# Six modulation vectors of a transformer block: one reduction moved from TensorE to VectorE, another into the feed-forward

## The chip, the cores and the metric

The kernel runs on one core of a Trainium2 chip. The core has five engines with a queue each: TensorE (PE, matrix products, with PEld as its weight load), VectorE (DVE), ScalarE (ACT), GpSimd (POOL) and SyncE (SP, which issues most transfers). Each queue is worked off in order; engines wait for each other by semaphores. The metric is the time of one execution on the device in microseconds.

## The reference

Two transformer blocks stand behind each other, for 256 tokens of width 1024, all in fp32. The first block has two kinds of attention (MoBA, and a gated delta rule that solves a triangular system), an output projection and a mixture of 32 experts with a router. The second block is modulated: six vectors of 1024 numbers are made from a condition `c` and are used as shift, scale and gate.

```python
mod = (jax.nn.silu(c) @ w_mod[l] + b_mod[l])[:, None, :]
mod_c = (jax.nn.silu(c_ctx) @ w_mod[l] + b_mod[l])[None, None, :]
sh1, sc1, g1, sh2, sc2, g2 = jnp.split(mod, N_MOD, axis=-1)
csh1, csc1, cg1, csh2, csc2, cg2 = jnp.split(mod_c, N_MOD, axis=-1)
h = _modulate(_rms_norm(x, norm1_g[l]), sh1, sc1)      # h * (1 + scale) + shift
hc = _modulate(_rms_norm(ctx, norm1_g[l]), csh1, csc1)
...
h2 = _modulate(_rms_norm(x_new, norm2_g[l]), sh2, sc2)
x = x_new + g2 * _swiglu(h2, w_gate[l], w_up[l], w_down[l])
```

The weight `w_mod` has 1024 x 6144 numbers, 24 MB. Of the six vectors of the context condition only the first two (shift and scale of the first norm) reach an output, so vectors 2 to 5 are needed for one condition alone. The hidden layer of the feed-forward has 2816 columns, which are worked through as 11 blocks of 256.

## The kernel before, in words

Weights come in blocks of 1 MB ([128, 2048] fp32) into a ring of nine slots (`load_block`); SP issues the loads in the order of use, and a load waits until its slot is free. For the exact products a block is split into a high and a low part (`split_w`): ACT writes the high part in two pieces of 1024 columns, DVE the low part in four of 512 (for some blocks POOL does). A product is then three matmuls (`mm3`).

Stage a makes the projections of block 1 while the delta rule's triangular inverse goes on. The inverse is a chain of short steps. First a loop over four heads makes the matrices `pkq` (a product of the keys `kn` with keys and queries), from which DVE makes `BT` and `QT`. Then seven levels follow, for two halves (`blk`) by turns: PE makes `pu`, DVE multiplies by a mask (`U`), PE multiplies again, DVE subtracts (`T`) and transposes (`W`); the last two levels have copies (`X`, `T64`, `Wf`) instead. Behind the levels come products `py` and `pb` with copies `yy` and a subtraction `vt`. The matmuls of this chain are short and each waits for DVE; so that PE has work, `fill(n)` puts `FILL[n]` steps of the projections (one `mm3` each) between them. From `PE.start()` on, which stands ahead of the levels, PE's order is as written; the other engines' order is made by a scheduler from the program, with `after(a, b)` as a bare order (a stands behind b on its engine, no semaphore).

The six modulation vectors are a generator, `mod_steps`, that yields after each weight block. `more_mod(n)` advances it by n yields; `MODS[:14]` says by how many after each projection, `MODR` after each level, `MODS[14:]` after each step of MoBA. A vector is four blocks of 1 MB. For each, PE takes the silu'd condition (`sil`, 32 columns: two conditions, 16 copies each) as weights and multiplies 256 columns at a time into four column groups of one PSUM tile, `pmod`: 32 matmuls a vector. Then DVE transposes it (line 397), adds the bias (line 398), and for the two scales multiplies by the norm's gain (line 400). All of it goes on in stage a, from the first projections to the end of the levels.

Stage c (router and experts, 96 MB of weights) follows, then stage d, block 2. In its feed-forward `ffn_up(b)` makes gate and up products `pfg` and `pfu` of a hidden block (48 matmuls each, on weights `fg` and `fu`, split into `fgh`, `fgl`, `fuh`, `ful`), ACT the silu (`fsg`, line 1801), DVE the product; `ffn_down(b)` multiplies by `fd` into four accumulators `pf`. The input is made by `mod_T`: DVE scales (`mt`, line 1470), ACT shifts into the high part (`hif`, line 1471), DVE makes the low part (`lof`, line 1472), for eight slices. The last gate g2 has to lie along the free axis, equal in all rows: `row_bc` makes that by 8 matmuls (`prb`) and two copies on ACT (`g2B`, line 1526), ahead of the first `ffn_up`; with `RBH` the copies stand behind the last `hif`.

Of the kernel before, what the change touches and what calls it, by code (L numbers as in the profile page):

```python
# [9 lines left out]
F32 = mybir.dt.float32  # L10
# [3 lines left out]
ALU = mybir.AluOpType  # L14
# [3 lines left out]
P = 128  # L18
D = 1024
# [86 lines left out]
def tile_kernel(ctx: ExitStack, tc: tile.TileContext, I, out, dbg=None):  # L106
# [99 lines left out]
    def bc(ap, n):  # L206
        return ap[..., None].to_broadcast(list(ap.shape) + [n])
# [172 lines left out]
    def mod_steps():  # L380


        for n in range(6):
            p = psm([P, 256], "pmod", "mo")
            wm = w_mod[:, n * D:n * D + D].rearrange("(p k) c -> p k c", k=8)
            for i in range(4):
                w = load_block(wm[:, 2 * i:2 * i + 2], "wmod")
                for kk in range(2):
                    for j in range(4):
                        m = PE.matmul(p[32 * j:32 * j + 32], lhsT=sil[:, 2 * i + kk].rearrange("p a b -> p (a b)"),  # L390
                                  rhs=w[:, kk, 256 * j:256 * j + 256], start=i + kk == 0, stop=i + kk == 4)
                        if kk + j == 0:
                            S_["mod"] = S_["mod0"] = m
                if i < 3:
                    yield
            part = tmp_([P, 8, 32], "part", "part")
            DVE.transpose(part, p.rearrange("p (c k) -> p k c", k=8))
            DVE.tensor_tensor(mod[:, n], part[:, :, 0::16], bc(bmc[:, n], 2), op=ALU.add)
            if n in (1, 4):
                DVE.scalar_tensor_tensor(mod[:, n], mod[:, n], 1.0, bc((gN1, gN2)[n // 4], 2), op0=ALU.add, op1=ALU.mult)  # L400
            yield

    MODA = MODS[:14]
# [3 lines left out]
    def more_mod(n=1):  # L407
        on, PE.on = PE.on, False
        for _ in range(n):
            before = S_.get("mod")  # L410
            next(mods, None)
            if S_.get("mod") is not before:
                if S_["nmod"] < MBEH and "pj1" in S_:
                    after(S_["mod0"], S_["pj1"])
                S_["nmod"] += 1
        PE.on = on
# [170 lines left out]
    for h in range(4):  # L587
# [8 lines left out]
        for dst, rr in ((BT[:, :, h], kn), (QT[h], gT["q", h])):  # L596
# [4 lines left out]
            DVE.scalar_tensor_tensor(dst[:, 0:2], src[:, 0:2], bt[:, 0, h:h + 1], dec[h][:, 0:2], op0=ALU.mult, op1=ALU.mult)  # L601
            DVE.scalar_tensor_tensor(dst[:, 2], src[:, 2], bt[:, 1, h:h + 1], dec[h][:, 2], op0=ALU.mult, op1=ALU.mult)

# [25 lines left out]
    def level(blk, n):  # L629
# [14 lines left out]
        Wn = ic("W")  # L644
        DVE.transpose(Wn.rearrange("p a b -> p (a b)"), Tn.rearrange("p a b -> p (a b)"))
        T[blk], W[blk] = Tn, Wn
# [27 lines left out]
    def level_64(blk):  # L674
# [3 lines left out]
        X = T64[blk]  # L678
        DVE.tensor_copy(X[64:128], px[64:128])
        yield  # L680
# [35 lines left out]
    fill(9)  # L716
    DVE.tensor_copy(yy[1], py)
    ob = aa([P, 2, 4, P], "zg", "ob", bufs=2)
# [1050 lines left out]
    pow_ins = S_["pow"]  # L1769

    with tc.issue_after(S_["rp"].ins):
        g2B = row_bc(mod[:, 5, :, 0], ring_tile("g2B", F32)[:, 0:D], ("mo", "sm"))
    if RBH:
        for i in S_["rbc"]:
            after(i, S_["hin"])
    rb_ins = S_["rb"]

    mt_ins, sq_ins, lo_ins = S_["mt"], S_["sq"], S_["lo"]
# [38 lines left out]

    prev = ffn_up(0)
    for b in range(1, 12):
        nxt = ffn_up(b) if b < 11 else None  # L1820
        ffn_down(b - 1, *prev)
        prev = nxt
# [9 lines left out]

MODR = [2, 2, 2, 2, 2, 2]
MODS = [0, 1, 2, 0, 1, 0, 1, 0, 2, 2, 2, 2, 2, 1, 0, 0, 0, 0]
IFU = 4
# [19 lines left out]
IC = 8  # L1855
FILL = [3] * 7 + [6] * 5 + [0, 2, 2]
START = 2
# [18 lines left out]
JKA = (True, True)  # L1876
RBH = True

# [28 lines left out]
```

## Time and profile before

| what | value |
|---|---|
| time, median of 3 runs | 831.15 us (830.29 to 833.35) |
| profiled execution | 835.07 us, span 833.3 us |
| mean granted clock of TensorE | 0.959 of full speed |
| PE busy | 758.9 us, 91% |
| PEld busy | 608.6 us, 73% |
| DVE busy | 425.8 us, 51% |
| ACT busy | 302.0 us, 36% |
| POOL busy | 108.2 us, 13% |
| moved by DMA | 201.21 MB, mean 241 GB/s |

The shares are means over stages with different limits; the table of stretches among the rows below shows them apart. A row of the timeline reads: start, busy time, engine, line, operation, output and input names, shape, how many instructions, and in brackets how long the engine was idle before it and whom it waited for. Matmuls overlap in the pipe, so pace is read from starts. Each fp32 matmul leaves two records (`x384` for the 192 matmuls of pmod); those of split parts leave one.

### The profile page before, as it was taken

Reading aid. Unit: us, or ns where it says so; the run is one execution under the profiler, and the core shown is the slowest. Engines: PE = TensorE matmul, PEld = TensorE weight load, DVE = VectorE, ACT = ScalarE, POOL = GpSimd, SP = SyncE. Lnnn points to the kernel's source line nnn. Section 1 sums busy time; section 2 is a strip of 40 time slices with the busy share of each in tenths; the row PEclk is TensorE's granted clock in tenths of the full one; section 3 lists DMA queues with packets and bytes.
Section 4 is the critical chain, followed back from the end, with each engine's and each line's share of the span. In section 5 each row is a group of like instructions: output and inputs, shape, how many; then the busy total and the mean of one; then the engine's idle time right before and its main releaser. Section 6 shows DMA issues by size and latency. Waiting matters only on the chain.

```text
span 833.3 us, 15024 instructions
## 1 busy us (share of the span) xinstructions
PE 758.9 (91%) x6276; PEld 608.6 (73%) x6276; DVE 425.8 (51%) x938; ACT 302.0 (36%) x533; POOL 108.2 (13%) x94
## 2 busy tenths in 40 slices
PE   7999999999799878697888999799988999999997
PEld 6887887966645425274654889688867999999996
DVE  4766553564612114003224788888655545545545
ACT  5532233443410010001114554488525343443441
POOL 5011000152000000000000566300122000000000
PEclk9999999999799989799898999799998999999999
DMA  7999778577589999999998317011442654655201
GB/s 213 357 386 390 283 280 298 203 288 319 206 341 419 420 417 419 391 409 409 409 396 284 116 22 206 2 51 52 152 152 79 225 197 161 199 187 171 97 2 50
DMA packets 87590, 201.21 MB, mean 241 GB/s; under 512 B 15496, under 2 KB 63040, under 8 KB 75232
## 3 DMA queue, kind: packets, MB, share of 16 engines
q1 hardware_dynamic: 87328, 200.12, 65.1%
q8 instruction: 50, 0.82, 0.4%
q0 software_dynamic: 192, 0.11, 0.1%
q14 instruction: 20, 0.16, 0.1%
HBM read 199.27 MB, written 1.05 MB: 240 GB/s over the span
## 4 chain that ended last, share of the span: by engine, by line
PE 39%; DMA 6%; DVE 6%; issue 3%; POOL 2%; ACT 1%; SPq 1%; DVEq 0%; POOLq 0%; ACTq 0%
PE pfu L99 8%; PE pfg L99 7%; PE pf L99 7%; PE sc L99 3%; DMA ed<-in_w_down_dram 3%; DMA kv<-in_w_in_dram 2%; PE po L99 2%; PE ptp L102 2%; PE pyd L99 2%; PE pqa L99 1%; PE pqb L99 1%; POOL rq L218 1%; PE ckbp L99 1%; PE pgu L99 1%; DMA lat<-in_w_in_dram 1%
## 5 line engine op out<-in xcount | busy, mean ns | idle before, releaser
L99 PE MATMUL pfu<-hif,fuh 128*128 128x256 f32 x176 | 50.7, 288 | 1.6 <-ACT fuh L185 1.6
L99 PE MATMUL pfu<-hif,ful 128*128 128x256 f32 x176 | 50.7, 288 | 0.9 <-POOL ful L192 0.9
L99 PE MATMUL pfu<-lof,fuh 128*128 128x256 f32 x176 | 50.6, 287 | 0.0
L99 PE MATMUL pyd<-ed,hid 128*32 128x512 f32 x256 | 42.0, 667 | 7.1 <-DMA ed<-in_w_down_dram 2.4
L99 PE MATMUL pfg<-hif,fgh 128*128 128x256 f32 x160 | 45.7, 286 | 0.0
L99 PE MATMUL pfg<-lof,fgh 128*128 128x256 f32 x160 | 45.7, 285 | 0.0
L99 PE MATMUL pfg<-hif,fgl 128*128 128x256 f32 x160 | 45.6, 285 | 0.0
L192 DVE TENSOR_TENSOR fdl<-fd,fdh 128x512 fp32r<-128x512 f32 x44 | 27.5, 687 | 28.9 <-ACT fdh L185 28.9
L99 PE MATMUL pgu<-eu,xg 128*32 128x256 f32 x512 | 35.7, 402 | 3.9 <-DMA eu<-in_w_up_dram 3.9
L1377 ACT ACTIVATE sg<-pgu,r1s 128x256 f32<-128x256 f32 x8 | 3.8, 474 | 94.7 <-PE pgu L99 70.9
L99 PEld LDWEIGHTS pfu<-hif,fuh 128*128 128x128 f32 x176 | 34.6, 197 | 1.8 <-ACT fuh L185 1.8
L185 ACT ACTIVATE fuh<-fu 128x1024 fp32r<-128x1024 f32 x22 | 22.1, 1052 | 38.2 <-issue 28.6
L99 PE MATMUL pgu<-eg,xg 128*32 128x256 f32 x512 | 34.2, 385 | 1.6 <-DVE sg L1378 1.1
L185 ACT ACTIVATE fdh<-fd 128x1024 fp32r<-128x1024 f32 x22 | 22.1, 1052 | 36.9 <-issue 36.1
L99 PEld LDWEIGHTS pfu<-hif,ful 128*128 128x128 f32 x176 | 34.6, 196 | 1.1 <-POOL ful L192 1.1
L99 PE MATMUL pf<-fdl,fh 128*128 128x512 f32 x88 | 35.1, 399 | 0.0
L1404 DVE TENSOR_TENSOR yl<-pyd,yh 128x512 fp32r<-128x512 f32 x16 | 11.1, 691 | 46.3 <-ACT yh L1403 35.9
L99 PE MATMUL pf<-fdh,fh 128*128 128x512 f32 x88 | 34.7, 394 | 0.0
L99 PEld LDWEIGHTS pfu<-lof,fuh 128*128 128x128 f32 x176 | 34.6, 197 | 0.0
L99 PE MATMUL pf<-fdh,fl 128*128 128x512 f32 x88 | 34.0, 392 | 0.0
L99 PEld LDWEIGHTS pyd<-ed,hid 128*32 128x32 f32 x256 | 9.7, 120 | 33.2 <-issue 22.0
L192 DVE TENSOR_TENSOR fgl<-fg,fgh 128x512 fp32r<-128x512 f32 x40 | 27.7, 753 | 9.1 <-ACT fgh L185 9.1
(716 smaller groups left out, 2185.2 us busy)
## 6 DMA issues: line engine op xcount, KB each, us to landing
eg<-in_w_gate_dram SPq DMA_DIRECT2D x32, 1024.0 KB, 17.5
eu<-in_w_up_dram SPq DMA_DIRECT2D x32, 1024.0 KB, 19.8
ed<-in_w_down_dram SPq DMA_DIRECT2D x32, 1024.0 KB, 15.4
wmod<-in_w_mod_dram SPq DMA_DIRECT2D x24, 1024.0 KB, 10.6
fg<-in_w_gate_dram SPq DMA_DIRECT2D x11, 1024.0 KB, 5.4
fu<-in_w_up_dram SPq DMA_DIRECT2D x11, 1024.0 KB, 5.3
fd<-in_w_down_dram SPq DMA_DIRECT2D x11, 1024.0 KB, 5.0
kv<-in_w_in_dram SPq DMA_DIRECT2D x5, 1024.0 KB, 15.2
```

The costliest lines, as they stand in the source:

```text
L99: return self._keep(self.engine.matmul(*args, **kwargs))
L102: return self._keep(self.engine.transpose(*args, **kwargs))
L185: S_["hi"] = ACT.activation(hf[:, s], vf[:, s], AF.Copy)
L192: i = (POOL if c in pool else DVE).tensor_tensor(lf[:, s], vf[:, s], hf[:, s], op=ALU.subtract)
L218: S_["pow"] = POOL.tensor_tensor(r, v, mhalf[:, :n], op=ALU.pow)
L1377: ACT.activation(sg, pgu[:, 0], AF.Silu, scale=r1s[:, u:u + 1])
L1404: DVE.tensor_tensor(yl, py, yh, op=ALU.subtract)
```

## The change

Vectors 0 and 1 (both conditions) stay on PE. Vectors 2, 3 and 4 go by `mod_sum`: DVE multiplies the first row block by its number of the condition in place (`TENSOR_SCALAR`, line 414 of the new kernel), and adds each other row block times its number to it (`SCALAR_TENSOR_TENSOR`, line 416): 128x512 each, 16 a vector. The first weight block's own slot holds the sums, so it stays taken until the vector is done. Then the 128 partitions are summed by 8 matmuls with one column of ones (`pmod`, [128, 8]), and the bias is added (line 431, 433). The first sum of each block is put behind the last step of the chain by `after` (`S_["hold"]`, which is set to the last of `BT`/`QT`, `W`, `X`, `yy`). Vector 5 is summed by the same `mod_rows` inside the feed-forward, one block at each of b = 3, 4, 5 and 6; at b = 7 two matmuls of 128x512 with ones sum the partitions and spread the result over all rows, and DVE adds a bias row that a broadcast transfer has brought. `row_bc` for g2 and `RBH` go. `MODR`, `MODS` and the first seven of `FILL` change: from the third level on four steps of the projections instead of three stand at each place.

```diff
 
-        for n in range(6):
+        for n in range(5):
+            if n > 1:
+                yield from mod_sum(n)
+                continue
             p = psm([P, 256], "pmod", "mo")
...
             DVE.tensor_tensor(mod[:, n], part[:, :, 0::16], bc(bmc[:, n], 2), op=ALU.add)
-            if n in (1, 4):
-                DVE.scalar_tensor_tensor(mod[:, n], mod[:, n], 1.0, bc((gN1, gN2)[n // 4], 2), op0=ALU.add, op1=ALU.mult)
+            if n == 1:
+                DVE.scalar_tensor_tensor(mod[:, n], mod[:, n], 1.0, bc(gN1, 2), op0=ALU.add, op1=ALU.mult)
             yield
+    def mod_rows(n, i, acc):
+
+        w = load_block(w_mod[:, n * D:n * D + D].rearrange("(p k) c -> p k c", k=8)[:, 2 * i:2 * i + 2], "wmod")
+        for kk in range(2):
+            for c in range(2):
+                cs = slice(512 * c, 512 * c + 512)
+                f = sc2t[:, 0, 2 * i + kk:2 * i + kk + 1]
+                if i + kk == 0:
+                    S_["sum0"] = DVE.tensor_scalar(w[:, 0, cs], w[:, 0, cs], f, None, op0=ALU.mult)
+                else:
+                    m = DVE.scalar_tensor_tensor((acc or w)[:, 0, cs], w[:, kk, cs], f, (acc or w)[:, 0, cs], op0=ALU.mult, op1=ALU.add)
+                    if kk + c == 0:
+                        S_["sum0"] = m
+        return acc or w
+
+    def mod_sum(n):
+
+        acc = None
+        for i in range(4):
+            acc = mod_rows(n, i, acc)
+            if i < 3:
+                yield
+        p = psm([P, 8], "pmod", "mo")
+        for k in range(8):
+            PE.matmul(p[:, k:k + 1], lhsT=acc[:, 0, k::8], rhs=ones1, start=True, stop=True)
+        DVE.tensor_tensor(mod[:, n, :, 0], p, bmc[:, n], op=ALU.add)
+        if n == 4:
+            DVE.scalar_tensor_tensor(mod[:, n, :, 0], mod[:, n, :, 0], 1.0, gN2, op0=ALU.add, op1=ALU.mult)
+        yield
 
...
-            before = S_.get("mod")
+            before, sum_ = S_.get("mod"), S_.get("sum0")
             next(mods, None)
+            if S_.get("sum0") is not sum_ and "hold" in S_:
+                after(S_["sum0"], S_["hold"])
...
         Wn = ic("W")
-        DVE.transpose(Wn.rearrange("p a b -> p (a b)"), Tn.rearrange("p a b -> p (a b)"))
+        S_["hold"] = DVE.transpose(Wn.rearrange("p a b -> p (a b)"), Tn.rearrange("p a b -> p (a b)"))
...
-    with tc.issue_after(S_["rp"].ins):
-        g2B = row_bc(mod[:, 5, :, 0], ring_tile("g2B", F32)[:, 0:D], ("mo", "sm"))
-    if RBH:
-        for i in S_["rbc"]:
-            after(i, S_["hin"])
-    rb_ins = S_["rb"]
-
+    g2 = ring_tile("g2B", F32)
+    g2B, b2B = g2[:, 0:D], g2[:, D:2 * D]
...
     prev = ffn_up(0)
+    acc = None
     for b in range(1, 12):
         nxt = ffn_up(b) if b < 11 else None
+        if b in GB:
+            if acc is None:
+                bcast_dma(b2B, I["b_mod_2"][0, 5 * D:6 * D], D)
+            acc = mod_rows(5, GB.index(b), acc)
+        if b == GB[-1] + 1:
+            for nh in range(2):
+                ns = slice(nh * 512, nh * 512 + 512)
+                p = psm([P, 512], "pg2", ("mo", "sm")[nh])
+                PE.matmul(p, lhsT=ones1.to_broadcast([P, P]), rhs=acc[:, 0, ns], start=True, stop=True)
+                DVE.tensor_tensor(g2B[:, ns], p, b2B[:, ns], op=ALU.add)
         ffn_down(b - 1, *prev)
...
-MODR = [2, 2, 2, 2, 2, 2]
-MODS = [0, 1, 2, 0, 1, 0, 1, 0, 2, 2, 2, 2, 2, 1, 0, 0, 0, 0]
+MODR = [1, 1, 1, 1, 1, 1]
+MODS = [0, 1, 2, 1, 1, 1, 1, 1, 0, 0, 1, 1, 2, 2, 0, 0, 0, 0]
...
-FILL = [3] * 7 + [6] * 5 + [0, 2, 2]
+FILL = [3, 3, 4, 4, 4, 4, 4] + [6] * 5 + [0, 2, 2]
...
-RBH = True
+GB = (3, 4, 5, 6)
```

The new lines `S_["hold"] = ...` stand in the same way at `QT`, `X` and `yy`.

The order on DVE in the inverse. Before, at the level where `wmk1` is split (L634 is `U`, L643 `T`, L645 `W`, L397 the vectors' transposition):

```order
L634 TENSOR_TENSOR U<-pu,lvl 128x128 x2
L543 SCALAR_TENSOR_TENSOR zg<-zg,wz1p 128x2x256
L643 TENSOR_TENSOR T<-T,pu 128x128
L555 TENSOR_TENSOR zg<-zg,gnorm 128x1024
L192 TENSOR_TENSOR wmk1l<-wmk_1456,wmk1h 128x512
L645 STREAM_TRANSPOSE W<-T 128x128
L192 TENSOR_TENSOR wmk1l<-wmk_1456,wmk1h 128x512
L397 STREAM_TRANSPOSE part<-pmod 128x256
L192 TENSOR_TENSOR wmk1l<-wmk_1456,wmk1h 128x512 x2
L643 TENSOR_TENSOR T<-T,pu 128x128
L398 TENSOR_TENSOR mod<-part,bmc 128x16
L645 STREAM_TRANSPOSE W<-T 128x128
```

After, at the end of the levels (L719 is `Wf`, the sums L414 and L416, L742 the copy `yy`, L431 the bias of a vector):

```order
L416 SCALAR_TENSOR_TENSOR wmod<-wmod,sc2t 128x512 x2
L719 TENSOR_SCALAR Wf_916<-pu 64x4x64
L416 SCALAR_TENSOR_TENSOR wmod<-wmod,sc2t 128x512 x3
L719 TENSOR_SCALAR Wf_920<-pu 64x4x64
L416 SCALAR_TENSOR_TENSOR wmod<-wmod,sc2t 128x512 x3
L192 TENSOR_TENSOR wmv1l<-wmv_1873,wmv1h 128x512 x2
L416 SCALAR_TENSOR_TENSOR wmod<-wmod,sc2t 128x512
L192 TENSOR_TENSOR wmv1l<-wmv_1873,wmv1h 128x512 x2
L416 SCALAR_TENSOR_TENSOR wmod<-wmod,sc2t 128x512
L742 COPY yy_1766<-py 128x512
L416 SCALAR_TENSOR_TENSOR wmod<-wmod,sc2t 128x512 x3
L431 TENSOR_TENSOR mod<-pmod,bmc 128x8
```

One to three sums stand in front of each step of the chain; in the rows before, only splits, the gate `zg` and the vectors' short steps stand between.

The order on ACT at the start of the feed-forward, where `jk` is the sum of squares of x, before:

```order
L1763 ACTIVATE jk,sq_6199<-x 128x512 x3
L1471 ACTIVATE hif<-mt,mod 128x256 x8
L1526 ACTIVATE g2B<-prb 128x4x128 x2
L1801 ACTIVATE fsg<-pfg 128x512
L185 ACTIVATE fuh<-fu 128x1024 x2
L185 ACTIVATE fgh<-fg 128x1024 x2
L185 ACTIVATE fuh<-fu 128x1024 x2
```

And after:

```order
L1798 ACTIVATE jk,sq_6125<-x 128x512 x3
L185 ACTIVATE fuh<-fu 128x1024 x2
L185 ACTIVATE fgh<-fg 128x1024 x2
L1506 ACTIVATE hif<-mt,mod 128x256 x8
L1830 ACTIVATE fsg<-pfg 128x512
L185 ACTIVATE fuh<-fu 128x1024 x2
L1834 ACTIVATE fh<-fsg 128x512
```

The high part `fuh` of the first up block and `fgh` now stand ahead of `hif`, and the copies to `g2B` are gone.

## Rows read from the trace of the kernel before

**Rows 1.** Table by stage: window, us, busy per engine (count), PEclk, DMA share, GB/s

```profile
20.00:80.56 60.56, 59.61 (x560) 49.33 (x559) 43.07 (x120) 25.15 (x54) 5.60 (x5) 1.00 1.04 377
80.56:164.00 83.44, 82.75 (x1053) 71.41 (x1054) 38.73 (x89) 27.11 (x50) 3.11 (x4) 1.00 0.77 276
240.00:450.00 210.00, 175.50 (x1495) 98.52 (x1492) 47.34 (x99) 23.08 (x42) 4.98 (x4) 0.93 0.99 401
630.00:826.00 196.00, 192.23 (x1323) 178.88 (x1322) 102.15 (x164) 80.97 (x96) 5.90 (x4) 0.98 0.42 140
```

**Rows 2.** The same table for tile pmod alone (PE, PEld, DVE)

```profile
80.56:145.00 64.44, 14.87 (x192) 6.10 (x192) 1.75 (x4) 1.00 0.82 291
104.88:147.23 42.35, 10.20 (x134) 4.25 (x134) 1.34 (x3) 1.00 0.83 291
```

**Rows 3.** Timeline of PE in the loop over heads

```profile
69.23 0.92 PE L99 MATMUL pkq<-kn 128*128 128x256 f32 x4
...
71.97 0.92 PE L99 MATMUL pkq<-kn 128*128 128x256 f32 x4 [0.71 <-DVE kn L594]
...
73.92 1.07 PE L99 MATMUL pmod<-wmod,sil 128*32 128x256 f32 x16
74.92 0.92 PE L99 MATMUL pkq<-kn 128*128 128x256 f32 x4
```

**Rows 4.** Timeline of PE at the one-column product psq

```profile
618.93 0.52 PEld L99 LDWEIGHTS psq<-ones,osq 128*128 128x128 f32 x4 [0.71 <-ACT osq L1665]
618.93 0.60 PE L99 MATMUL psq<-ones,osq 128*128 128x1 f32 x4 [0.47 <-ACT osq L1665]
```

**Rows 5.** Groups of DVE by line: shape, count, busy us, mean ns, idle before

```profile
L1636 DVE TENSOR_SCALAR prb<-prb,st 128x512 f32<-128x512 f32 x16 | 7.7, 481 | 0.1
L543 DVE SCALAR_TENSOR_TENSOR zg<-zg,wz0p 128x512 f32<-128x512 f32 x1 | 0.7, 689 | 1.2 <-ACT zg L542 1.2
```

**Rows 6.** Timeline of DVE from the third level to yy

```profile
98.16 2.50 DVE L192 TENSOR_TENSOR wmk0l<-wmk,wmk0h 128x512 fp32r<-128x512 f32 x4
...
104.88 0.31 DVE L645 STREAM_TRANSPOSE W<-T 128x128 f32<-128x128 f32 x1
...
147.23 0.69 DVE L707 COPY yy<-py 128x512 f32<-128x512 f32 x1 [3.37 <-PE py L99]
```

**Rows 7.** Table by stretch after the wait

```profile
644.00:646.00 2.00, 2.00 (x12) 2.00 (x11) 2.00 (x2) 0.25 (x1) 2.00 (x3) 0.50 1.06 370
```

**Rows 8.** Timeline at the start of the feed-forward

```profile
630.34 1.30 ACT L1471 ACTIVATE hif<-mt,mod 128x256 fp32r<-128x256 f32 x3 [3.80 <-DVE mt L1470]
...
630.90 0.38 PE L99 MATMUL pfg<-hif,fg0h 128*128 128x256 f32 x1
...
636.46 0.39 PE L99 MATMUL pfg<-lof,fg0h 128*128 128x256 f32 x1
...
639.87 0.60 ACT L1801 ACTIVATE fsg<-pfg 128x512 f32<-128x512 f32 x1 [1.96 <-PE pfg L99]
...
640.36 2.00 ACT L185 ACTIVATE fuh<-fu 128x1024 fp32r<-128x1024 f32 x2
...
641.47 0.39 PE L99 MATMUL pfu<-hif,fuh 128*128 128x256 f32 x1 [1.63 <-ACT fuh L185]
...
642.82 0.58 PE L99 MATMUL pfu<-hif,ful 128*128 128x256 f32 x1 [0.85 <-POOL ful L192]
```

**Rows 9.** The chain of waits: start, us, what

```profile
657.08 5.76 PE pfu L99 x48
```

**Rows 10.** POOL's timeline at the feed-forward's start; DVE's group beside its splits

```profile
627.61 0.71 POOL L218 TENSOR_TENSOR rf<-rfv,mhalf 128x2 f32<-128x2 f32 x1 [2.43 <-DVE rfv L216]
641.49 5.90 POOL L192 TENSOR_TENSOR ful<-fu,fuh 128x512 fp32r<-128x512 f32 x4 [13.18 <-ACT fuh L185]
...
L192 DVE TENSOR_TENSOR fgl<-fg,fgh 128x512 fp32r<-128x512 f32 x4 | 5.2, 1358 | 6.9 <-ACT fgh L185 6.9
```

**Rows 11.** The chain of waits at an earlier row broadcast

```profile
559.29 1.09 PE prb L99 x8
```

**Rows 12.** Transfers: line, queue, count, KB each, median us to landing

```profile
wmod<-in_w_mod_dram SPq DMA_DIRECT2D x24, 1024.0 KB, 10.6
```

More of the change, by code (lines that the diff above doesn't have):

```diff
@@ L601, in tile_kernel @@
             DVE.scalar_tensor_tensor(dst[:, 0:2], src[:, 0:2], bt[:, 0, h:h + 1], dec[h][:, 0:2], op0=ALU.mult, op1=ALU.mult)
-            DVE.scalar_tensor_tensor(dst[:, 2], src[:, 2], bt[:, 1, h:h + 1], dec[h][:, 2], op0=ALU.mult, op1=ALU.mult)
+            S_["hold"] = DVE.scalar_tensor_tensor(dst[:, 2], src[:, 2], bt[:, 1, h:h + 1], dec[h][:, 2], op0=ALU.mult, op1=ALU.mult)
     BD = []
@@ L678, in level_64 @@
         X = T64[blk]
-        DVE.tensor_copy(X[64:128], px[64:128])
+        S_["hold"] = DVE.tensor_copy(X[64:128], px[64:128])
         yield
@@ L716, in tile_kernel @@
     fill(9)
-    DVE.tensor_copy(yy[1], py)
+    S_["hold"] = DVE.tensor_copy(yy[1], py)
     ob = aa([P, 2, 4, P], "zg", "ob", bufs=2)
```

## The prediction

> **What bounds the kernel now.** I read the stretches first, then the removed instructions alone, then the order of the work where they stood, and last the chain of waits at the start of the feed-forward. In the table of stretches the reader is to see three different kernels [rows 1]. From 20 us to 164 us (projections and triangular inverse of block 1) PE is busy 59.61 of 60.56 us and 82.75 of 83.44 us at a granted clock of 1.00: PE sets the time, and DVE is busy only 46% of the second stretch (38.73 of 83.44). From 240 to 450 us the transfers set it (DMA share 0.99). From 630 to 826 us PE is busy 192.23 of 196.00 us, and DVE 102.15. What PE loses before 164 us reaches the end: the weights of the experts that fill the middle are loaded into ring slots that come free only when the earlier stages have used theirs, so that block starts earlier by as much as its predecessors end earlier. Half of the modulation stands in the PE-bound stretch: between 80.56 and 145 us 192 records with 14.87 us are pmod [rows 2]. One vector is 32 matmuls of two records each, so this is three vectors at 4.96 us.
>
> **The change part by part.** *Removed before the inverse.* The loop over the heads that makes pkq had one vector's matmuls between its turns. The rows show a turn without them, 69.23 to 71.97 = 2.74 us with 0.71 us of idle time for DVE's kn, and one with them, 71.97 to 74.92 = 2.95 us [rows 3]. So the matmuls mostly stood in a gap that will be empty: about 0.2 us a turn, four turns, I take -1.0 us. Bounds 0 (the gap takes all) and -4.96 (all of it was on the path).
>
> *Removed and added on PE in the inverse.* -14.87 us [rows 2]. Added are three times 8 matmuls of one column with 128 columns of weights. The nearest row is psq, 128x1 too: four records took 0.52 us to load and 0.60 us to run [rows 4]. 16 records a vector at 0.13 are 2.1 us, 6.3 us in all; at 0.15 they are 7.2; if the load hid wholly behind neighbours they would be near 0. I take +6.3, the row's own pace. The twelve projection matmuls between steps, nine before, are the same work earlier, so nothing in the sum.
>
> *Added on DVE in the inverse.* Each vector is 2 TENSOR_SCALAR and 14 SCALAR_TENSOR_TENSOR of 128x512. The nearest rows are 0.48 us (0.689 us for the fused form) [rows 5]; four queued splits of the same size took 2.50 us, so 0.61 us from start to start where none waits [rows 6]. From the third level's second transposition to the first yy, 104.88 to 147.23 us, the old path is 42.35 us [rows 6], of which 10.20 were pmod [rows 2]. In the new order 33 fused sums and 4 plain ones stand in that stretch of DVE's queue, beside 20 splits and some 20 short steps of the inverse. The sums are 33 x 0.61 + 4 x 0.4 = 21.7 us, the splits 20 x 0.61 = 12.2, zg 1.8, the short steps some 5 (20 of 0.25): 41 us, or 43 with 0.69 for the sums. PE's side of the same stretch is 42.35 - 10.20 + 48 matmuls more (four levels by four gaps by three) at 0.12, the pace of 48 pfu in 5.76 us [rows 9] (5.8) + 2 x 2.1 = 42.2 us. DVE, idle for half of this stretch before, becomes as long as PE, and everything that PE does with the inverse passes through DVE twice a level. Two queues of equal load that wait for each other by turns don't both run full. Where it shows last: the 8 matmuls of the third vector stand ahead of pb on PE and need the sum that is last on DVE before yy; behind them on PE are pb, the second py and the projections of the values. Bounds: 0, if the lags cancel, and +11, which is a quarter of the stretch. Holding each block's first sum behind W, X or yy keeps it from delaying that step, but a sum of 0.61 us that has started stands in front of whatever arrives during it: some 20 short steps with half a sum each (0.3) are 6 us, not all of it on PE's path. I take +5.
>
> The row shows four splits 0.61 us apart though each lasts 0.69 [rows 6]. [...]
>
> *Added wait and the clock.* [...] Two microseconds at half clock lose one; I take +1 us, bounds 0 and +4 (four such stretches).
>
> *The start of the feed-forward.* Before, the row broadcast of g2 (16 records of prb) stood before the first pfg, and its two copies on ACT after hif. That put the first gate, fsg, at 639.87 and the weights' high half, fuh, at 640.36, although these weights had long been loaded; PE waited 1.63 us until 641.47 and again 0.85 until 642.82 [rows 8]. Now fuh and fgh come ahead of hif, in the 3.80 us that ACT sat idle before hif [rows 8], and pfu stands between the pfg steps. So the first two blocks' 192 matmuls, which took from 630.90 to 657.08 + 5.76 = 662.84, or 31.9 us [rows 8, 9], lose their waits and most of the slow clock. 192 at 0.12 us are 23.0 us. Four conversions of 1.0 us each are 4.0, so hif is at most 0.4 late. While PE still follows the chain mt, hif, lof (to 636.46 [rows 8]), 43 of the 192 are done; 149 at 0.12 are 17.9 us, so 654.8 at the earliest, -8.0. POOL's four splits of fuh, 5.90 us, now run beside this chain; beside them DVE's splits took 1.358 us a piece instead of 0.69 [rows 6, 10]. If they halve the pace of mt and lof from 629.7 to 634.2 (5.9 us behind rf's end at 628.3 [rows 10]), the chain is 2.2 us longer, -5.8. If nothing but the first wait goes, -2. The matmuls of prb kept PE active ahead of it, and the clock may be lower without them; I take -5.
>
> *The last vector inside the feed-forward.* Two matmuls of 128x512: four of 128x128, the same 512 columns, took 1.09 us [rows 11], so +2.2. Its sixteen sums (11 us of DVE at 0.69) and two additions lie in a stretch where DVE is busy 52% [rows 1]: at nothing. If that cover were gone, a sum would delay fgl or fdl by 0.7 us a block, +3. The four 1 MB loads and the bias's broadcast share 16 engines at a DMA share of 0.42 [rows 1]: at nothing too, since the weights are loaded several blocks ahead.
>
> **The sum** against the profiled execution (835.07 us, of which 833.3 is the span): -1.0 - 14.9 + 6.3 + 5 + 1 - 5 + 2.2 = -6.4, so 828.7. That execution is 3.9 us above the median of the runs; against the median of 831.15 it is 824.7.
>
> **The rivals.** *The vector queue becomes the bound of the inverse (slower).* The sum of DVE is already 41 to 43 us against PE's 42.2, and the sums also need weights that land 10.6 us after issue [rows 12], while the sum's own block keeps a ring slot of 1 MB for three more, so splits in DVE's in-order queue can stand behind a sum whose block is not there. With the upper bounds for wait and clock (+11, +4) and -2 for the feed-forward: -1.0 - 14.9 + 6.3 + 11 + 4 - 2 + 2.2 = +5.6, or 836.8. It decides once PE's waits and slower clock in the inverse exceed 9.4 us (12.4 if the feed-forward still gives 5), and by more than 0.5% four beyond that. Against it: transfers take a share of only 0.77 there, and they have fallen behind nothing, as PE's idle time of 0.69 us in 83.44 shows [rows 1]. [...]
>
> *No change.* PE's removed work covered waits that remain: those in the inverse are 9 instead of 5, and the feed-forward gives 3 instead of 5: -0.4, or 830.8. For it: the loop over heads shows how little a removed matmul gives where DVE is awaited [rows 3]. Against it: in the inverse DVE had half of its time free [rows 1].
>
> *Twice the gain.* DVE's sums fit its gaps, +0.5, the clock stays at its higher level and the feed-forward's start gives 8: -1.0 - 14.9 + 6.3 + 0.5 - 8 + 2.2 = -14.9, or 816.3. For it: DVE was free for more than half of the inverse [rows 1]. Against it: the sums and splits together fill that half.
>
> That the edit doesn't do what it says can be excluded by the order of the instructions: the 128 pmod matmuls of four vectors are gone from PE.
>
> **How the numbers follow.** The forecast has a chance of 0.42, the gain of 15 us 0.14, no change 0.26, the slower case 0.18. The forecast's own range is 820 to 830: the wait from +1 to +9, the start of the feed-forward from -3 to -7. About 0.5% (4.2 us) is what a measurement of this kernel can tell from no change. Faster by more than that: 0.14 and nearly all of the forecast, 0.41, so 0.55. Slower by more: 0.17 of the slower case. Within: 0.28. The range of 8 in 10 goes from 815, below the larger gain, to 836, into the slower case.
>
> **What would show it.** In the inverse: PE idle time before the one-column pmod and before pu and pb, with DVE's sums as what precedes it; DVE busy near all of the stretch from W to yy; the experts' stretch as long as before but earlier. In the feed-forward: first pfu right behind the first pfg, no fsg ahead of fuh, the two blocks' last matmul 5 us nearer to the first. The forecast is wrong if DVE is idle for much in the inverse (then 816), if PE's idle time there is above 9 us, or if the experts don't start earlier by what the inverse saves.

## The result, and the profile after

The changed kernel takes 837.13 us (median of 9 runs, 834.16 to 840.08) where the kernel before took 831.15: a ratio of 1.0069, 95% interval [1.0051, 1.0088]. It is slower by some 6 us; the forecast was 6.4 us faster. The profiled execution took 836.16 us (span 834.4), 1.0 us under the median of its runs; that of before took 835.07, 3.9 us above its median, so the two profiles show less of the difference than the runs do.

The table by stage, columns as in [rows 1], of the changed kernel:

```profile
20.00:80.56 60.56, 56.45 (x504) 48.65 (x504) 44.42 (x122) 24.75 (x54) 7.31 (x7) 1.00 1.00 359
80.56:164.00 83.44, 79.24 (x863) 75.63 (x862) 61.26 (x120) 24.65 (x46) 0.43 (x1) 0.90 0.58 202
240.00:450.00 210.00, 174.16 (x1559) 99.14 (x1554) 48.56 (x105) 23.60 (x42) 4.97 (x4) 0.95 1.02 412
630.00:826.00 196.00, 193.23 (x1331) 180.32 (x1330) 113.63 (x187) 79.12 (x96) 5.83 (x5) 0.98 0.48 159
```

Against [rows 1] DVE went from 38.73 to 61.26 us in the inverse. From the third level's second transposition to the first yy it was busy 43.70 of 50.07 us, where the prediction had worked out 41 to 43 us. PE lost 3.5 us of busy time, and its granted clock fell from 1.00 to 0.90: 8.3 us of full speed, where the forecast had 1. The first expert product shows what the stages ahead came to (tile rows: ns min/median/max, first and last start), of before and then of after:

```profile
L99 PE MATMUL pgu<-eg,xg x512: 379/379/637, 224.1 to 433.9; 128*32 128x256 f32 x171
```

```profile
L99 PE MATMUL pgu<-eg,xg x512: 378/380/633, 232.9 to 440.2; 128*32 128x256 f32 x171
```

8.8 us late, where the forecast had it about 3.6 early (its terms ahead of the feed-forward). On DVE the loss comes late in the inverse: the second transposition of the third level is 4.8 us earlier than in [rows 6] (100.09 against 104.88), yet the first yy is 2.9 us later and the second 9.3. The first fence is the second yy before (a tile row), the other DVE's timeline after:

```profile
L717 DVE COPY yy<-py x1: 692/692/692, 153.3 to 153.3; 128x512 f32<-128x512 f32 x1
```

```profile
100.09 0.31 DVE L680 STREAM_TRANSPOSE W<-T 128x128 f32<-128x128 f32 x1
...
100.68 2.07 DVE L416 SCALAR_TENSOR_TENSOR wmod<-wmod,sc2t 128x512 f32<-128x512 f32 x3
...
150.16 0.69 DVE L742 COPY yy<-py 128x512 f32<-128x512 f32 x1
...
162.65 0.69 DVE L752 COPY yy<-py 128x512 f32<-128x512 f32 x1 [3.35 <-PE py L99]
```

PE's waits between 80 and 172 us are only these (waited for: us in total, times, longest); the DVE queue that I feared shows as 2.0 us, for Wf and T. The wait for vt comes from ACT's order: a split of wmv1 of 2.00 us stands ahead of vt there.

```profile
PE pv L102 <- ACT vt L736: 2.2, 1, 2.2
PE pu L99 <- DVE Wf L719: 1.1, 1, 1.1
PE pu L99 <- DVE T L678: 0.9, 1, 0.9
```

The rest is in the one-column matmuls and behind them. PE's timeline at the first group, then the table of the four stretches around it:

```profile
123.09 3.85 PE L99 MATMUL pmod<-ones,wmod 128*128 128x1 f32 x16
126.80 0.56 PE L99 MATMUL wmq0p<-htl,wmq0h 128*128 128x256 f32 x1
```

```profile
120.00:124.00 4.00, 4.00 (x43) 3.81 (x40) 3.71 (x7) 2.89 (x6) 0.00 (x0) 1.00 1.06 371
124.00:128.00 4.00, 4.00 (x18) 3.92 (x18) 2.30 (x6) 0.00 (x0) 0.00 (x0) 0.84 0.31 120
128.00:132.00 4.00, 4.00 (x62) 3.57 (x60) 2.46 (x5) 0.92 (x3) 0.00 (x0) 0.50 0.96 328
132.00:136.00 4.00, 4.00 (x42) 3.73 (x35) 2.67 (x5) 2.13 (x4) 0.00 (x0) 0.81 0.60 200
```

A group takes 3.71 us to the next matmul, not 2.1, and the clock then stands at 0.50 while PE is busy in every microsecond: no wait came first. These 12 us lose 0.16 x 4 + 0.50 x 4 + 0.19 x 4 = 3.4 us of full speed. The second group (from 151.89) also takes 3.71 us and loses as much. With the third (from 172.32) it is 5.1 us, but there PE also waits, for ob and mixh; another 1.7 us are lost behind the wait for vt, which ends at 147.30. From 124 to 192 us that makes 13.6 us. One slice of 4 us behind the second group and one behind the third:

```profile
156.00:160.00 4.00, 4.00 (x20) 4.00 (x20) 0.69 (x1) 0.00 (x0) 0.00 (x0) 0.50 0.91 313
176.00:180.00 4.00, 2.86 (x12) 1.28 (x13) 3.80 (x9) 0.00 (x0) 2.66 (x3) 0.50 0.69 240
```

The feed-forward's start, as forecast, against [rows 8 to 10]:

```profile
630.16 1.99 ACT L185 ACTIVATE fuh<-fu 128x1024 fp32r<-128x1024 f32 x2
...
632.00 5.15 POOL L192 TENSOR_TENSOR ful<-fu,fuh 128x512 fp32r<-128x512 f32 x4
...
633.95 1.29 ACT L1506 ACTIVATE hif<-mt,mod 128x256 fp32r<-128x256 f32 x3
634.47 2.96 DVE L1507 SCALAR_TENSOR_TENSOR lof<-mt,mod,hif 128x256 fp32r<-128x256 f32 x2
634.49 0.39 PE L99 MATMUL pfg<-hif,fg0h 128*128 128x256 f32 x1 [1.71 <-ACT hif L1506]
...
636.06 0.58 PE L99 MATMUL pfg<-lof,fg0h 128*128 128x256 f32 x1 [1.06 <-DVE lof L1507]
```

```profile
656.04 5.76 PE pfu L99 x48
```

The second fence is the chain of waits. From the first pfg to the end of the second block: 656.04 + 5.76 - 634.49 = 27.3 us, 31.9 before: -4.6. Two lof beside POOL's splits took 2.96 us (0.87 before), the stretching that I had allowed for. The slow clock, which the prediction wanted mostly gone, stayed: 0.50 from 636 to 642 us now and from 644 to 648 before, and by slices of 2 us 3.4 us of full speed are lost either way. What went is waits.

### The profile page after: what moved, and what is told of

Same layout as the page of the kernel before. It is cut to its first block, busy times and chain, and to the rows that moved or that the text cites. A ratio compares the mean times of both kernels' runs of the same rounds, so it can differ in the third digit from the quotient of the medians.

```text
span 834.4 us, 14657 instructions
## 1 busy us (share of the span) xinstructions
PE 756.5 (91%) x6056; PEld 618.2 (74%) x6056; DVE 466.0 (56%) x999; ACT 299.6 (36%) x531; POOL 108.0 (13%) x94
## 4 chain that ended last, share of the span: by engine, by line
PE 40%; DMA 6%; DVE 6%; POOL 2%; issue 1%; ACT 1%; SPq 1%; DVEq 0%; POOLq 0%; ACTq 0%
PE pfg L99 8%; PE pfu L99 8%; PE pf L99 7%; PE sc L99 3%; DMA ed<-in_w_down_dram 3%; DMA kv<-in_w_in_dram 2%; PE po L99 2%; PE ptp L102 2%; PE ckbp L99 2%; PE pyd L99 1%; PE pqa L99 1%; PE pqb L99 1%; POOL rq L218 1%; PE pgu L99 1%; DMA lat<-in_w_in_dram 1%
## 5 line engine op out<-in xcount | busy, mean ns | idle before, releaser
L416 DVE SCALAR_TENSOR_TENSOR wmod<-wmod,sc2t 128x512 f32<-128x512 f32 x56 | 40.8, 759 | 0.3
L1439 DVE TENSOR_TENSOR yl<-pyd,yh 128x512 fp32r<-128x512 f32 x16 | 11.1, 691 | 43.6 <-ACT yh L1438 36.3
L99 PE MATMUL pgu<-eu,xg 128*32 128x256 f32 x512 | 32.8, 381 | 1.7 <-DMA eu<-in_w_up_dram 1.7
## 6 DMA issues: line engine op xcount, KB each, us to landing
eg<-in_w_gate_dram SPq DMA_DIRECT2D x32, 1024.0 KB, 16.3
```

The source lines that it names most:

```text
L99: return self._keep(self.engine.matmul(*args, **kwargs))
L416: m = DVE.scalar_tensor_tensor((acc or w)[:, 0, cs], w[:, kk, cs], f, (acc or w)[:, 0, cs], op0=ALU.mult, op1=ALU.add)
L1439: DVE.tensor_tensor(yl, py, yh, op=ALU.subtract)
```

## The experiments

The kernel before ran beside each, on the same chip; ratios are to it, with 95% intervals. A ratio of 0.01 is 8.3 us. They come in the order in which they ran.

**wide.** 64 columns of ones instead of one.

```diff
-            PE.matmul(p[:, k:k + 1], lhsT=acc[:, 0, k::8], rhs=ones1, start=True, stop=True)
+            PE.matmul(p[:, k], lhsT=acc[:, 0, k::8], rhs=ones1.to_broadcast([P, 64]), start=True, stop=True)
```

> The changed kernel (837.1 us, profiled span 834.4), but each of the 24 sums over partitions multiplies by 64 columns of ones instead of one; the extra columns aren't read. Theory A: the one-column matmuls themselves drop TensorE's granted clock to its lower level (13.6 us of full-speed time lost between 124 and 192 us), because so little moves through the engine while they run. Then with 64 columns the clock stays at 1.00 in this stretch though the matmuls last as long (3.7 us a vector); the second yy comes at 156 instead of 162.7, the time is 826 to 830. Rival B: the clock falls because of PE's waits for DVE's sums and transfers. Then the same dips remain and the time stays at 835 to 839.

1.0046 [1.0012, 1.0080]: not told from the changed kernel. The second yy came at 157.5, and the clock fell for some 3 us behind the first group (0.87 and 0.70 in the slices of 4 us from 124 to 132 us) and again behind the third, where PE waits too (0.50 from 172 to 180 us), but not behind the second (1.00 from 132 to 168 us). The scheduler also moved that group six matmuls up, so this run does not decide; add64 asks it cleanly.

**nomm.** No one-column matmuls.

```diff
-        p = psm([P, 8], "pmod", "mo")
-        for k in range(8):
-            PE.matmul(p[:, k:k + 1], lhsT=acc[:, 0, k::8], rhs=ones1, start=True, stop=True)
-        DVE.tensor_tensor(mod[:, n, :, 0], p, bmc[:, n], op=ALU.add)
+        DVE.tensor_tensor(mod[:, n, :, 0], acc[:, 0, 0:8], bmc[:, n], op=ALU.add)
```

> The changed kernel without the 24 one-column matmuls: the vectors 2 to 4 take eight columns of the sums as they are (the sum over partitions is left out). DVE's sums, transfers and holds stay. Theory A: 3 x 3.7 us of PE and the dips of the clock go, 11 + 8 to 10 us: 816 to 820, second yy near 147. Rival B (DVE's queue is the bound of the inverse): PE's waits for DVE remain and are longer; the gain is at most 4: 833 to 837.

0.9982 [0.9952, 1.0013]: 7 us less, between the two. PE now waits 4.8 us for DVE's ob (pto), 1.8 for vt, and 5.1 for Wf (1.6 of it on ACT), T and X. Theory A overrated the groups by leaving out what they had covered.

**nosum.** No sums on DVE but the first product of each vector.

```diff
-                    m = DVE.scalar_tensor_tensor((acc or w)[:, 0, cs], ...)
-                    if kk + c == 0:
-                        S_["sum0"] = m
+                    if n == 5:
+                        DVE.scalar_tensor_tensor((acc or w)[:, 0, cs], ...)
```

> The changed kernel without 42 of the 48 sums on DVE for the vectors 2 to 4: of each vector only the first row block is multiplied and summed over partitions, the other sums are left out (the weights are still loaded). Theory A: the one-column matmuls and the dips of the clock remain; only the waits of PE for DVE (1.1 for Wf, 0.9 for T, some 1.5 more for vt) go: 833 to 836, the granted clock still 0.5 after each of the three groups. Rival B: DVE bounds the inverse, so some 9 us or more come back: 826 to 829.

1.0110 [1.0055, 1.0164]: no gain. The scheduler then puts all three groups into the levels, ahead of the first yy (157.1); PE is busy throughout up to 152 us and waits 4.8 us for ob later. While the groups are there, taking DVE's work away gave nothing; what the groups' new places did to this run is not told apart from it.

**ffn_only.** The kernel before with the new feed-forward alone: `mod_rows`, `for n in range(5)` and the hunks with `g2`, `acc` and `GB`; `MODR`, `MODS` and `FILL` stay.

> The kernel before with only vector 5 moved into the feed-forward (sums on DVE there, two matmuls of 128x512); vectors 2 to 4 stay on PE as before, levels and FILL as before. One vector's 32 matmuls (4.96 us) leave the inverse, the start of the feed-forward is 4.6 us shorter as in the changed kernel, its inside 1.7 us longer: 831.15 - 7.9 = 823. If the gain at the start of the feed-forward is lost later, or the removed matmuls were cover for waits, 828 to 831.

0.9899 [0.9868, 0.9931], 823.8 us: as expected, and faster than both kernels. So vectors 2 to 4 on DVE cost 0.0170, some 14 us.

**add1, add64.** The kernel before with three groups added, which nothing waits for (64 columns in the second).

```diff
         if n:
             more_mod(MODR[n - 1])
+        if n in (2, 4, 6):
+            padd = psm([P, 8, 1], "padd")
+            for k in range(8):
+                PE.matmul(padd[:, k], lhsT=x[:, 0, k::8], rhs=ones1, start=True, stop=True)
```

> The kernel before with three groups of 8 matmuls more, of one column of ones and 128x128 weights read with a stride of 8 from x, behind the third, fifth and seventh level; nothing reads their result. No wait and no DVE work is added. Theory A (the one-column matmuls drop the granted clock): 3 x 3.8 us for the groups and some 3 us of full-speed time lost in a dip to 0.50 behind each: +20, about 852. Rival B (the clock fell for PE's waits): the clock stays 1.00 as in the kernel before, +11, about 843.

> The same three groups of 8 matmuls added to the kernel before, with 64 columns of ones instead of one. Theory A: the groups last as long, 3.8 us each, and the clock stays at 1.00: about 843, some 9 us under the one-column version. Rival B: the same as the one-column version.

1.0181 [1.0149, 1.0212] and 1.0206 [1.0177, 1.0236]: +15.0 and +17.1 us. For add1 that is between A's +20 and B's +11, and add64 came no lower. In the inverse both lose over 20 us (the second yy at 174.3 and 173.7, 153.3 before); some 3 to 6 of them do not reach the end. PE at the first group of add1, and the table of stretches behind it, of add1 and then of add64:

```profile
105.58 3.85 PE L99 MATMUL padd<-ones,x 128*128 128x1 f32 x16
109.29 1.04 PE L99 MATMUL pu<-T,BD 128*128 128x32 f32 x4
```

```profile
104.00:108.00 4.00, 4.00 (x55) 3.94 (x52) 0.60 (x2) 0.00 (x0) 0.00 (x0) 1.00 1.02 404
108.00:112.00 4.00, 4.00 (x19) 4.00 (x19) 0.29 (x1) 0.00 (x0) 0.00 (x0) 0.63 0.03 8
112.00:116.00 4.00, 4.00 (x20) 4.00 (x20) 0.29 (x1) 0.35 (x1) 0.00 (x0) 0.50 0.00 0
```

```profile
108.00:112.00 4.00, 4.00 (x20) 4.00 (x19) 0.00 (x0) 0.00 (x0) 0.00 (x0) 0.82 0.33 130
112.00:116.00 4.00, 4.00 (x20) 4.00 (x20) 0.29 (x1) 0.00 (x0) 0.00 (x0) 0.50 0.00 0
116.00:120.00 4.00, 4.00 (x47) 3.71 (x48) 2.28 (x4) 2.49 (x3) 0.00 (x0) 0.50 0.00 0
```

No wait, no DVE work, and the clock still goes to 0.50: rival B is out for the fall of the clock. The part of theory A that blamed the single column is out too, since 64 columns fall as deep.

**rowsum.** Two matmuls of 512 columns per vector.

```diff
+        for nh in range(2):
+            p = psm([P, 512], "pmod", ("mo", "sm")[nh])
+            PE.matmul(p, lhsT=ones1.to_broadcast([P, P]), rhs=acc[:, 0, 512 * nh:512 * nh + 512], start=True, stop=True)
+            DVE.tensor_tensor(mod[:, n, 4 * nh:4 * nh + 4, 0], p[:, 0:4], bmc[:, n, 4 * nh:4 * nh + 4], op=ALU.add)
```

> The changed kernel with the sum over partitions of vectors 2 to 4 made by two matmuls of 128x512 each with ones as weights (as the changed kernel does for vector 5); of the result, which lies along the free axis, eight columns are taken (so those vectors are not the reference's). Theory A: 2.2 us a vector instead of 3.7, no dip of the clock that isn't behind a wait: 824 to 829. Rival B: as changed, 835 or more. A third theory, C, that with PE's filler gone the inverse is bound by the latency of its chain through DVE and ACT: PE's waits in the inverse grow by what the matmuls save, 830 to 834.

0.9936 [0.9916, 0.9957], 829.57 us; by the ratio 825.8, in theory A's range. The same sums on DVE, in the levels the same two waits for them (T 0.9, Wf 0.3 us), and by the ratios 11 us less than the changed kernel, although PE now waits 4.0 us for ob: that is the price of the form of the matmuls.

**none.** nosum and nomm together.

> The changed kernel with neither the 42 further sums on DVE nor the 24 one-column matmuls of vectors 2 to 4 (these vectors are left out but for 6 plain multiplications; their weights are loaded). Without the matmuls but with the sums it was 830.3. If DVE's sums make PE wait once the matmuls are gone (B), this gains some 10 us more: 818 to 821. If the chain's own latency is the bound (C), PE's waits stay and it is 828 to 831.

0.9886 [0.9843, 0.9930]. Against nomm 8 us less: DVE's sums do cost, once the groups are gone. But with all work of vectors 2 to 4 gone this is no better than ffn_only, which has it on PE: theory C in part, and none_fill3 below shows why.

**add1c, add1s.** add1 with contiguous weights (the edit is shown against add1); the 24 strided matmuls one by one in the kernel before.

```diff
-                PE.matmul(padd[:, k], lhsT=x[:, 0, k::8], rhs=ones1, start=True, stop=True)
+                PE.matmul(padd[:, k], lhsT=x[:, 0, k * P:k * P + P], rhs=ones1, start=True, stop=True)
...
                 fill(n)
+                if n:
+                    padd = psm([P, 8], "padd")
+                    PE.matmul(padd[:, 0:1], lhsT=x[:, 0, n::8], rhs=ones1, start=True, stop=True)
```

> The kernel before with the same three groups of 8 one-column matmuls added (+15 us with weights read at a stride of 8), but with contiguous columns of x as weights. Nothing waits for them. Theory A1: the pace of the strided weight load (0.24 us a record against 0.13 of the contiguous psq) is what makes a group long and TensorE slow enough in its work to lose its clock; then a group takes 2.1 us, the dips are gone or shorter, +5 to +8. Rival A2: any run of such weights with few columns drops the clock; then the dips to 0.50 stay, +12 or more.

> The kernel before with the same 24 strided one-column matmuls added, but one by one, one behind each of the 24 places where the inverse of the levels two to seven has its projection matmuls. Theory A1: without a run of them the clock stays at 1.00, so they cost their own 24 x 0.47 = 11 us at most, +8 to +11 (part of it in gaps). Rival: each of them slows what follows, and it stays at +15.

1.0096 [1.0061, 1.0131] and 1.0156 [1.0127, 1.0185]. The load of one record (tile rows of add1, then of add1c) and the stretches of add1c, then of add1s:

```profile
L99 PEld LDWEIGHTS padd<-ones,x x48: 312/335/337, 105.5 to 162.3; 128*128 128x128 f32 x48
```

```profile
L99 PEld LDWEIGHTS padd<-ones,x x48: 192/192/192, 106.9 to 153.4; 128*128 128x128 f32 x48
```

```profile
108.00:112.00 4.00, 4.00 (x32) 4.00 (x32) 0.29 (x1) 0.00 (x0) 0.00 (x0) 0.83 0.42 166
112.00:116.00 4.00, 4.00 (x48) 3.71 (x48) 1.59 (x4) 2.49 (x3) 0.00 (x0) 0.50 0.00 0
```

```profile
108.00:112.00 4.00, 4.00 (x67) 3.17 (x67) 0.60 (x2) 0.00 (x0) 0.00 (x0) 1.00 1.04 382
112.00:116.00 4.00, 4.00 (x32) 3.45 (x32) 0.39 (x2) 0.00 (x0) 0.00 (x0) 1.00 0.51 202
```

The stride of 8 makes a load 0.335 us instead of 0.192. Contiguous groups still lose the clock behind the first two (0.50 above, then 0.82 and 0.75 from 132 to 140 us) and hold it behind the third (1.00 from 140 to 224 us); single ones hold it throughout the levels (1.00 in every slice of 4 us from 88 to 164 us) but cost more than their 11 us (the second yy is 16.3 us late), so spreading them gains little. add1c lies at the edge of A1's "+5 to +8"; add1s is above it.

**drop.** ffn_only without vectors 2 to 4 (loads kept).

```diff
+            if n > 1:
+                for i in range(4):
+                    load_block(w_mod[:, n * D:n * D + D]..., "wmod")
+                    if i < 3:
+                        yield
+                DVE.tensor_copy(mod[:, n], bc(bmc[:, n], 2))
```

> The kernel in which only vector 5 was moved (0.990 of the kernel before), with the 96 matmuls of vectors 2 to 4 left out as well; these vectors are the bias alone, their weights are loaded and not read, and nothing is put in their place on DVE. If PE's busy time sets the inverse, as the prediction's first step has it, 14 us more go: 0.973 of before. If those matmuls were filler beside a chain that is as long without them (theory C), 0 to 4 us go: 0.985 to 0.990.

0.9785 [0.9735, 0.9835]: 9.5 us below ffn_only (good to some 5), between 14 and 4. The matmuls were mostly work, to a third cover.

**rb_late.** The kernel before with g2's broadcast at block 7.

```diff
-    with tc.issue_after(S_["rp"].ins):
-        g2B = row_bc(mod[:, 5, :, 0], ring_tile("g2B", F32)[:, 0:D], ("mo", "sm"))
...
+        if b == 7:
+            g2B = row_bc(mod[:, 5, :, 0], ring_tile("g2B", F32)[:, 0:D], ("mo", "sm"))
```

> The kernel before with only the row broadcast of g2 moved from ahead of the first hidden block to the seventh; all six vectors are made on PE as before. fuh and fgh then stand ahead of hif on ACT as in the changed kernel. If the 4.6 us at the start of the feed-forward come from that order, 0.994 of before, and the rest of the kernel with vector 5 alone moved (0.990) is its 32 matmuls. If it needs the absence of vector 5's work, 0.998 to 1.000.

0.9944 [0.9919, 0.9968]: as expected. By the medians more than half of ffn_only's gain is the order at the feed-forward's start and needs no sum.

**fill4, fill3.** FILL of the changed kernel in the one before, and the other way round.

```diff
-FILL = [3] * 7 + [6] * 5 + [0, 2, 2]
+FILL = [3, 3, 4, 4, 4, 4, 4] + [6] * 5 + [0, 2, 2]
```

> The kernel before with nothing but the changed kernel's FILL (four projection steps instead of three at each place from the third level on). My prediction put this move at nothing. If it takes filler from the tail of the inverse (vt, py, pb, ob), waits of some 5 us before pto and pv appear and a dip of the clock behind them: 1.005 to 1.010 of before. If the matmuls of the six vectors still cover the tail: 0.998 to 1.002.

> The changed kernel (1.007 of before) with FILL as before, three steps everywhere. If FILL's four steps strip the tail of its cover, some 6 us come back: 0.998 to 1.001. If the tail is covered by the one-column groups and DVE's sums bound the inverse, no change, 1.005 to 1.008, or slower, since fewer matmuls then stand beside the sums in the levels.

1.0039 [1.0016, 1.0062] and 1.0076 [1.0038, 1.0115]. It costs the old kernel 3 us, between the two ranges, with 4.8 us of wait for ob before pto; the changed kernel gains nothing from its undoing. There PE waited only 1.1 us for ob: the third group stands just ahead of it. But fill3 changed more than the cover: over 80 to 164 us the clock was 0.84, against 0.90 in the changed kernel. So it does not show what FILL costs at an equal clock.

```profile
80.00:164.00 84.00, 82.40 (x855) 78.13 (x855) 61.19 (x121) 25.85 (x48) 1.57 (x3) 0.84 0.49 165
```

**sum4, sum4_fill3.** A right and short sum over partitions, without and with the old FILL.

```diff
...
-        for k in range(8):
-            PE.matmul(p[:, k:k + 1], lhsT=acc[:, 0, k::8], rhs=ones1, start=True, stop=True)
...
+        for j in range(4):
+            PE.matmul(p[32 * j:32 * j + 32], lhsT=ones1.to_broadcast([P, 32]),
+                      rhs=acc[:, 0, 256 * j:256 * j + 256], start=True, stop=True)
+        part = tmp_([P, 8, 32], "part", "part")
+        DVE.transpose(part, p.rearrange("p (c k) -> p k c", k=8))
...
```

> The changed kernel with the 8 one-column matmuls of each of the vectors 2 to 4 replaced by 4 matmuls of 256 columns with 32 columns of ones as weights and the transposition on DVE that the kernel before has (0.45 us); it computes the same vectors. A group is 8 records of 0.08 us, 0.6 us, in place of 3.7. If the one-column groups (their length and the dips behind them) are what the changed kernel loses, 0.992 to 0.995 of before, as with the sum by two matmuls of 512 columns (0.994). If it is the DVE work, 1.003 to 1.007.

> Both: vectors 2 to 4 summed over partitions by 4 matmuls of 256 columns, and FILL as before. If both causes add up, 0.984 to 0.988, better than vector 5 alone moved (0.990). If DVE's sums are the bound once PE has less to do, 0.992 to 0.995.

0.9958 [0.9935, 0.9981] and 0.9930 [0.9910, 0.9950]: 828.84 and 827.08 us. The better sum turns the change into a gain of 0.4%; with DVE's sums in the inverse even the better version isn't ahead of ffn_only (0.9899), and the two causes do not add up.

**none_fill3, drop_mods.** none with the old FILL; drop with the new MODR and MODS.

> The kernel without the further sums and without the one-column matmuls of vectors 2 to 4 (0.989 of before), with FILL as before. If FILL's four steps are what separates it from the kernel that left out these vectors with the old tables (0.978), it comes to 0.977 to 0.981 and PE's waits for pto and pv go from 7.1 us to about 1.5. If it is the order of the vectors' steps (MODS, MODR), it stays at 0.986 to 0.990.

> The kernel with the old tables that leaves out vectors 2 to 4 (0.978 of before), with MODR and MODS of the changed kernel, FILL as before. If FILL is the difference, it stays at 0.977 to 0.981. If the place of the weights' loads in the stream (MODS, MODR) is, 0.985 to 0.990.

0.9785 [0.9749, 0.9822] and 0.9791 [0.9758, 0.9825]. The difference is FILL alone. PE's waits in none from 130 us on, the two stretches at the wait for ob and behind it, and the waits in none_fill3:

```profile
PE pto L102 <- DVE ob L780: 4.8, 2, 2.8
PE pv L102 <- ACT vt L732: 2.3, 1, 2.3
```

```profile
160.00:164.00 4.00, 0.60 (x3) 0.47 (x4) 4.00 (x8) 0.00 (x0) 2.87 (x3) 0.67 0.02 2
164.00:168.00 4.00, 3.31 (x12) 2.38 (x11) 2.69 (x13) 2.61 (x10) 0.00 (x0) 0.50 0.98 367
```

```profile
PE pv L102 <- ACT vt L732: 0.7, 1, 0.7
PE sc L99 <- DVE mv L580: 0.6, 1, 0.6
PE pto L102 <- DVE mst L837: 0.5, 1, 0.5
```

The fourth step at each place made the levels longer (the second yy at 146.8 us in none, 139.8 in none_fill3), and left the tail bare.

## Why the prediction was wrong

The runs make a chain from the kernel before to the changed one, each step a measured pair (intervals of these ratios are 0.2 to 0.5% wide on either side, so a step is good to some 3 to 5 us):

| step | pair | measured, us | predicted, us |
|---|---|---|---|
| vector 5 and the feed-forward | before, ffn_only | -8.4 | -7.8 (-4.96 - 5 + 2.2) |
| vectors 2 to 4 off PE | ffn_only, drop | -9.5 | -10.9 (-1.0 - 9.9) |
| FILL | none_fill3, none | +8.4 | 0 |
| DVE's sums | none, nomm | +8.0 | +5 |
| one-column groups and clock | nomm, after | +7.2 | +7.3 (6.3 + 1) |
| sum | | +5.7 | -6.4 |

drop and none_fill3 are both 0.9785, which closes the chain. Of the 12.1 us between forecast and result 8.4 are FILL and 3.0 DVE's sums. So in this order the step that failed is "the same work earlier, so nothing in the sum", a term put at nothing that measured 8.4 us. The chain's order matters, though, for the three costs cover each other. Undone in the changed kernel itself, FILL gives nothing (fill3), DVE's sums give nothing (nosum), and the form of the groups gives 9 us (sum4) to 11 (rowsum). So as the kernel stands, what it lost first is the groups, and the prediction failed there too. The holds were not undone on their own, and the new MODR and MODS were tried only where vectors 2 to 4 are left out (drop_mods, no difference), so what they do in the changed kernel is not shown. Term by term:

- *"The row's own pace" for the one-column matmuls (+6.3, from psq [rows 4]).* Mis-sized: 3 x 3.7 = 11.1 us. psq's weights are contiguous, these are read at a stride of 8 (0.335 against 0.192 us a load, add1 and add1c). That the two agree in the table is luck: nomm had lost the groups' cover as well, so the table has the net price.
- *"Added wait and the clock" (+1).* The size and the cause were wrong: 13.6 us of full speed were lost from 124 to 192 us, and only a part of that behind waits. No run shows by itself the two microseconds at half clock that the +1 stands on; they were my estimate. What the changed kernel showed in their place is 1.7 us of full speed lost behind the wait for vt, 6.8 behind the first two groups, where PE did not wait, and 5.1 with the third. The clock fell at each group, in add1 with PE busy throughout (0.50 from 112 to 116 us, PE 4.00 of 4.00), so waits alone do not describe this fall.
- *DVE's sums (+5).* Right in kind; 8 us where the groups don't hide them. Three of them took 2.07 us and one by itself 0.74, so they start about 0.66 apart, 0.08 before the one ahead has ended, as the splits do (0.69 long, 0.61 apart: four in 2.50 us [rows 6]).
- *The start of the feed-forward (-5) and its inside (+2.2).* Right in size: -4.6 in the trace, and rb_late has 0.9944 for the order alone. It came from the waits and not from the clock (3.4 us of full speed lost before and after). That the clock may be lower without prb's matmuls was my estimate: the first 2 us from the first pfg had 0.82 (634 to 636 us), and 1.00 before (630 to 632). From the first pf to the last it is 166.1 us against 164.4: +1.7.
- *What is saved ahead reaches the end.* Held in part. In the four kernels that only add work ahead (add1, add64, add1c, add1s) the second yy of the profile is 21.0, 20.4, 10.4 and 16.3 us later, and the runs are 15.0, 17.1, 8.0 and 13.0 us longer: 0.7 to 0.84 of it arrives. From the first expert product to the last it was 219.7 to 225.3 us over the profiles, with no pattern that I could name. That spread of 5 us is left open, and is why the runs decide here and not single spans.

The slower rival had the right sign and, by luck, the size (836.8), with the wrong mechanism: DVE's queue isn't what the changed kernel lost its time on. Of the prediction's signs of being wrong one came, the late experts; PE's idle time in the inverse was 4.2 us (83.44 - 79.24), not above 9.

## What to carry to other kernels

Price a replacement by the form of its operands (the stride of a weight load: 0.335 us against 0.192 here; how few columns follow each load: 1.0069 with 8 matmuls of one column, 0.9936 with two of 512), not by the nearest row of the same shape, and look at what the engine's clock does behind such a run even if nothing waits (0.50 in add1). In a chain with filler, a filler table is part of the critical path: taking filler earlier lengthens the levels and bares the tail, and the whole bill comes once other cover is gone (8 us there, 3 in the kernel before). Split a change that has two halves before judging it: here one half gained 1.0% and the other lost 1.7%.

## What the runs showed of the hardware that was not expected

- A run of 8 fp32 matmuls with 128x128 weights at a stride of 8 and 1 or 64 columns (0.335 us a load in both; 3.71 us the run in add1) was followed by a fall of the granted clock to 0.50 without any idle time (add1 and add64, 112 to 116 us, PE busy 4.00 of 4.00); single ones among other matmuls were not (1.00 throughout the levels in add1s). It did not fall behind every run: not behind the second of wide (1.00 from 132 to 168 us), nor behind the third of add1c, whose weights are contiguous (1.00 from 140 to 224 us). What decides it stays open.
- Weights of fp32 read at a stride of 8 elements loaded in 0.335 us, contiguous ones in 0.192. A strided group took 3.71 us whether the clock was at 1.00 (the first of the changed kernel) or fell to 0.50 during it (the second, from 154.0 us on), while contiguous loads went from 0.192 us (pb before) to 0.333 at 0.50 (pb after).
